# Moving the stores of the last two chunks from GpSimd's DMA queue to SyncE's

## Chip, cores, metric

One core of one Trainium2 chip. The metric is the device time in microseconds (us) of one execution. "Span" is the time from the first to the last instruction of the execution whose trace was kept; the device time is about 1.8 us longer than the span.

A DMA has "landed" when the last of the 16 DMA engines has updated its semaphore. A "DRAIN" here is an instruction that an engine's sequencer (the part that issues its instructions) runs at the program's end, before a closing barrier in which the engines wait for one another; the profile doesn't count it as busy time.

## The reference

```python
def setup_inputs():
    return {
        "pred": np.random.uniform(0.01, 0.99, (8192, 8192)).astype(np.float32),
        "target": np.random.randint(0, 2, (8192, 8192)).astype(np.float32),
    }

def reference(pred, target):
    eps = 1e-7
    pred = np.clip(pred, eps, 1 - eps)
    return -(target * np.log(pred) + (1 - target) * np.log(1 - pred))
```

It reads 537 MB and writes 268 MB, elementwise.

## The kernel before

The flat arrays are cut into chunks, and a chunk into 128 rows, one for each partition. `ring_p` and `ring_t` are rings of 32768 columns, two big chunks. A chunk is loaded whole. It is computed in pieces, in place in `ring_p`, and stored whole; only the last two chunks (`k >= tail`) are stored piece by piece. Loads of `target` cast float32 to bfloat16. Every DMA but the very first load of `pred` is issued by GpSimd.

```python
RING = 32768
BIG = 16384

def plan(total):
    head = [(8192, [4096, 4096]), (8192, [8192])]
    tail = [(8192, [4096, 4096]), (8192, [4096, 2048, 1024, 1024])]
    n = (total - sum(w for w, _ in head + tail)) // BIG
    chunks = head + [(BIG, [BIG // 2] * 2)] * n + tail
    ...
    return chunks, len(chunks) - len(tail)
# ... (tiles, dram(), span()) ...
    def load(k):
        queue = nc.sync if k == 0 else nc.gpsimd
        nc.gpsimd.dma_start(out=span(ring_t, cols[k], widths[k]), in_=dram(target_f, k))
        queue.dma_start(out=span(ring_p, cols[k], widths[k]), in_=dram(pred_f, k))

    def store(k, off, w):
        nc.gpsimd.dma_start(
            out=dram(out_f, k)[:, off : off + w], in_=span(ring_p, cols[k] + off, w)
        )

    def front(col, w):   # VectorE: clip, then (t - 1) + p; ScalarE: Abs, Ln
        ...
    def back(col, w):    # VectorE: times -1
        ...
    def finish_one():
        nonlocal stored
        k, off, w = waiting.pop(0)
        back(cols[k] + off, w)
        if k >= tail:
            store(k, off, w)
        elif off + w == widths[k]:
            store(k, 0, widths[k])
        else:
            return
        stored = cols[k] + off + w
        load_what_fits()
# ... (the loop: front() of a piece, then finish_one() of the piece before) ...
```

## Time and profile before

| | before |
|---|---|
| device time, median | 1871.96 us (1871.66 to 1872.73, 3 runs) |
| span of the traced execution | 1868.4 us (it took 1870.21 us, less than the 3 timed runs) |
| busy: VectorE (DVE), ScalarE (ACT) | 60%, 48% |
| DMA engines | 9 tenths or more in 39 of 40 slices |
| last store: issued, landed | 1852.85, 1863.37 us |
| closing DRAIN of GpSimd: from, to | 1852.83, 1867.70 us |

From the page of the kernel before: busy time, DMA in 40 slices (tenths), and the DMA queues. q0 is the software queue, which GpSimd feeds; q1 is the hardware queue, which SyncE feeds here.

```profile
DVE 1121.7 (60%) x208; ACT 899.7 (48%) x140; POOL 63.5 (3%) x109
...
DMA  9999999999999999999999999999999999999998
...
q0 software_dynamic: 15120, 666.90, 99.3%
q1 hardware_dynamic: 144, 4.19, 0.6%
```

The 16 DMA engines bound the kernel from start to end; compute has slack. So a change at the end can only act on how the end runs out.

The end of the timeline of the kernel before (start, duration, instruction):

```profile
1851.86 0.69 DVE L96 TENSOR_SCALAR ring_p<-ring_p 128x1024 f32<-128x1024 f32 x1 [1.61 <-ACT ring_p L92]
1852.85 0.53 POOL L79 DMA_DIRECT2D out_dram<-ring_p  x1 [1.77 <-DVE ring_p L96]
```

Nothing that the timeline counts happens after 1853.4 us, but the span ends at 1868.4. Ten of these 15 us are the transfer of the backlog of stores. For the rest one has to ask for the line of the program's end, L165 (count, duration in ns min/median/max, first and last start; a "q" after an engine's name means its sequencer):

```profile
L165 POOLq DRAIN  x3: 51/96/14875, 1852.8 to 1868.2; - x3
L165 SPq DRAIN  x3: 7/7/7, 1863.4 to 1868.0; - x3
```

One of GpSimd's closing DRAINs takes 14.875 us; SyncE's take 7 ns. And the waits of SyncE's queue (total us, times, longest):

```profile
SPq L165 <- DMA out_dram<-ring_p: 1862.1, 5, 1852.5
SPq L165 <- PEq L165: 4.8, 2, 4.4
```

SyncE waits for the stores, and then 4.4 us more in an end-of-program barrier. The view names PE there; the raw records of the trace show that GpSimd came last:

```
(us, the raw instruction records of before; DMA landing = 16th semaphore update)
1852.83  GpSimd DRAIN              14.875
1863.37  last store lands (all 16 DMA engines)
1863.49  Sync   DRAIN  0.007       SyncE reports to the barrier
1867.75  GpSimd EVENT_SEMAPHORE    the barrier goes on, after the DRAIN
1868.44  end of span
```

### The profile page before, as it was taken

How to read it: one execution, taken by the hardware profiler on the slowest of the kernel's cores; microseconds unless marked ns; L12 is line 12 of the kernel's file. 1: busy time of each engine (PE TensorE's matmuls, PEld its weight loads, DVE VectorE, ACT ScalarE, POOL GpSimd, SP SyncE). 2: the span in 40 equal slices, each digit the busy share in tenths (PEclk: the TensorE clock that was granted, in tenths of full speed). 3: DMA queues.
4: the chain of work that ended last, by engine and by line, in shares of the span. 5: the costliest groups of instructions: out<-in, count | busy, mean ns of one | idle time of the engine just before them, and what ended most of it. 6: DMA issues, size and time to landing. Idle time of an engine off the chain costs nothing.

```text
span 1868.4 us, 607 instructions
## 1 busy us (share of the span) xinstructions
DVE 1121.7 (60%) x208; ACT 899.7 (48%) x140; POOL 63.5 (3%) x109
## 2 busy tenths in 40 slices
DVE  4557665476654766547665566655666556675575
ACT  3355433554335543355533555335553345533465
POOL 1000000000000000000000000000000000000001
DMA  9999999999999999999999999999999999999998
GB/s 303 359 348 337 356 396 370 349 345 338 400 382 337 354 340 387 395 340 341 351 379 392 353 340 342 380 393 353 349 338 368 399 356 345 349 354 397 371 337 346
DMA packets 15268, 671.13 MB, mean 359 GB/s; under 512 B 1696, under 2 KB 1696, under 8 KB 1952
## 3 DMA queue, kind: packets, MB, share of 16 engines
q0 software_dynamic: 15120, 666.90, 99.3%
q1 hardware_dynamic: 144, 4.19, 0.6%
q14 instruction: 4, 0.03, 0.0%
HBM read 536.87 MB, written 268.44 MB: 431 GB/s over the span
## 4 chain that ended last, share of the span: by engine, by line
DMA 33%; issue 25%; ACT 24%; DVE 15%; POOL 1%; POOLq 0%; DVEq 0%; PEldq 0%
DMA ring_p<-in_pred_dram 31%; ACT ring_p L92 12%; ACT ring_p L91 12%; DVE ring_p L88 8%; DVE ring_p L85 4%; DVE ring_p L96 4%; DMA out_dram<-ring_p 1%; DMA ring_t<-in_target_dram 1%; POOL out_dram L79 1%; POOL ring_t L75 0%; POOLq L165 0%; POOLq L79 0%; DVEq L88 0%; PEldq L165 0%; POOLq L76 0%
## 5 line engine op out<-in xcount | busy, mean ns | idle before, releaser
L91 ACT ACTIVATE ring_p<-ring_p 128x8192 f32<-128x8192 f32 (+3 forms) x69 | 450.4, 6528 | 949.2 <-DVE ring_p L88 949.2
L88 DVE SCALAR_TENSOR_TENSOR ring_p<-ring_t,ring_p 128x8192 f32<-128x8192 bf16 (+3 forms) x69 | 557.1, 8074 | 2.5 <-DMA ring_t<-in_target_dram 0.2
L85 DVE TENSOR_SCALAR ring_p<-ring_p 128x8192 f32<-128x8192 f32 (+3 forms) x69 | 283.9, 4114 | 384.4 <-DMA ring_p<-in_pred_dram 384.4
L96 DVE TENSOR_SCALAR ring_p<-ring_p 128x8192 f32<-128x8192 f32 (+3 forms) x69 | 284.1, 4117 | 343.1 <-ACT ring_p L92 343.1
L92 ACT ACTIVATE ring_p<-ring_p 128x8192 f32<-128x8192 f32 (+3 forms) x69 | 450.9, 6535 | 2.2
L79 POOL DMA_DIRECT2D out_dram<-ring_p x38 | 27.4, 721 | 876.1 <-DVE ring_p L96 876.1
L76 POOL DMA_DIRECT2D ring_p<-in_pred_dram x33 | 17.6, 534 | 912.8 <-DMA out_dram<-ring_p 912.8
L75 POOL DMA_DIRECT2D ring_t<-in_target_dram x34 | 18.7, 549 | 0.8 <-PEq L165 0.8
L126 ACT ACT_TABLE_LOAD x1 | 1.3, 1283 | 0.7 <-PEq L154 0.7
L125 DVE MEMSET warm<- 1x8 f32 x1 | 0.1, 65 | 0.8 <-PEq L154 0.8
L126 ACT ACTIVATE warm<-warm 1x8 f32<-1x8 f32 x1 | 0.2, 208 | 0.0
L154 POOL MEMSET const-float32-0.0<- 128x1 f32 x1 | 0.1, 98 | 0.2 <-issue 0.2
L154 POOL MEMSET const-bfloat16-1.0<- 128x1 bf16 x1 | 0.1, 101 | 0.0
L154 POOL MEMSET const-float32-1.0<- 128x1 f32 x1 | 0.1, 98 | 0.0
L154 POOL MEMSET const-uint8-127<- 128x1 uint8 x1 | 0.1, 98 | 0.0
## 6 DMA issues: line engine op xcount, KB each, us to landing
ring_t<-in_target_dram POOLq DMA_DIRECT2D x30, 4096.0 KB, 50.0
ring_p<-in_pred_dram POOLq DMA_DIRECT2D x3, 4096.0 KB, 37.4
ring_t<-in_target_dram POOLq DMA_DIRECT2D x4, 2048.0 KB, 29.3
out_dram<-ring_p POOLq DMA_DIRECT2D x2, 4096.0 KB, 35.9
out_dram<-ring_p POOLq DMA_DIRECT2D x3, 2048.0 KB, 15.9
ring_p<-in_pred_dram SPq DMA_DIRECT2D x1, 4096.0 KB, 19.5
out_dram<-ring_p POOLq DMA_DIRECT2D x1, 1024.0 KB, 12.8
out_dram<-ring_p POOLq DMA_DIRECT2D x2, 512.0 KB, 11.1
```

The source lines that it names most:

```text
L75: nc.gpsimd.dma_start(out=span(ring_t, cols[k], widths[k]), in_=dram(target_f, k))
L76: queue.dma_start(out=span(ring_p, cols[k], widths[k]), in_=dram(pred_f, k))
L79: nc.gpsimd.dma_start(out=dram(out_f, k)[:, off : off + w], in_=span(ring_p, cols[k] + off, w))
L85: nc.vector.tensor_scalar(out=p, in0=p, scalar1=EPS, scalar2=1 - EPS, op0=Alu.max, op1=Alu.min)
L88: nc.vector.scalar_tensor_tensor(out=p, in0=t, scalar=1.0, in1=p, op0=Alu.subtract, op1=Alu.add)
L91: nc.scalar.activation(out=p, in_=p, func=Act.Abs)
L92: nc.scalar.activation(out=p, in_=p, func=Act.Ln)
L96: nc.vector.tensor_scalar(out=p, in0=p, scalar1=-1.0, scalar2=None, op0=Alu.mult)
L125: nc.vector.memset(warm, 1.0)
L126: nc.scalar.activation(out=warm, in_=warm, func=Act.Ln)
L154: nc = _bacc.Bacc("TRN2", target_bir_lowering=False, num_devices=1)
```

## The change

As the diff shows it: the stores of the last two chunks go out on another queue, SyncE's. The last two pieces become one.

```diff
-    tail = [(8192, [4096, 4096]), (8192, [4096, 2048, 1024, 1024])]
+    tail = [(8192, [4096, 4096]), (8192, [4096, 2048, 2048])]
@@
     def store(k, off, w):
-        nc.gpsimd.dma_start(
+        queue = nc.sync if k >= tail else nc.gpsimd
+        queue.dma_start(
             out=dram(out_f, k)[:, off : off + w], in_=span(ring_p, cols[k] + off, w)
         )
```

## The prediction

> **What bounds the kernel now.** The 16 DMA engines: the page's 40 slices show DMA at 9 tenths in all but the last, DVE busy 60%, ACT 48%. The change touches only the six stores of the last two chunks, so nothing before about 1812 us (the last full-chunk store) can move. In the tail I read three things.
>
> 1. *Data.* The DMA view shows 405 to 442 GB/s from 1812 to 1850. The raw packet records give 16 KB packets 611 ns, 8 KB 309, 4 KB 159. On the slowest DMA engine the last landings follow without a gap: big store 1843.9, tail stores 1848.7, 1853.6, 1858.4, 1860.9, 1862.1, 1863.4. Each step is eight packets of that engine (8 x 611 ns = 4.9 us), so its queue is never empty; the last store is issued at 1852.85 and lands 10.6 us later.
> 2. *Compute.* The timeline ends with VectorE at 1852.5, 11 us before the last byte: off the critical path.
> 3. *Closing.* SyncE sees the last landing and is done at 1863.5. But GpSimd's closing DRAIN starts at 1852.83 and takes 14.88 us, to 1867.71: 4.3 us after the last landing. The final barrier waits for it (in the waits of SyncE's queue, 4.4 us for an end-of-program barrier). Then come 0.7 us; the span is 1868.4.
>
> **What the change does.** Six stores leave GpSimd's software queue (0.53 to 2.03 us to issue each), and five go out on SyncE's hardware queue (its one load now: 0.37 us to issue, first packet 1.0 us after the issue began). The last two stores of 512 KB become one of 1 MB. The instruction order shows nothing else moved on GpSimd; SyncE's extra waits are for loads that landed by about 1825.
>
> Piece by piece:
> - Issue time saved: up to 2 us per store, behind a backlog: worth 0.
> - Merge: 8 x 309 against 16 x 159 ns per engine, -0.07 us. The last piece is ready later (1.22 + 2.29 + 1.89 + 1.91 + 1.22 us; estimate 1853.3 against 1852.5), behind a backlog that lasts to about 1861: 0.
> - Rate: the same 16 engines. The Trainium skill ("DMA: Bandwidth & Descriptors", section "Issuing engines are not separate DMA queues") says DMAs from any engine interleave on them; the trace agrees at the head, where 32 KB packets take a median of 1226 ns on the hardware and 1213 on the software queue. The tail stores will interleave with the big store, which lands later (estimate 1847 to 1850 instead of 1844); nothing waits for it. The sum is unchanged: last landing about 1863.4.
> - DRAIN: GpSimd's last transfer is now the big store. If DRAIN waits for the software queue's transfers plus about 4.3 us, it ends at about 1852 to 1854, hidden under the remaining stores. That takes 4.3 us off the critical path, less about 0.1 for the handover.
>
> **Time.** 1871.96 - 4.2 = 1867.8 us, range 1866.0 to 1870.8; faster by over 2%: 0.003, within 2%: 0.99, slower: 0.007. A gain of about 0.2%.
>
> **To check.** DRAIN starts near 1813 and ends before the last landing; last landing within 1 us of 1863.4; span ends under 1 us after it; the hardware queue carries 12.6 MB; the big store lands later; VectorE and ScalarE unchanged up to 1845.
>
> **What would make it wrong.** A closing cost of the same kind on SyncE; DRAIN's 4.3 us not tied to the software queue; slower or smaller packets in hardware-queue stores; or, on the good side, the straggling DMA engines (last landings spread over 4.3 us) being evened out by the other queue.

## The result

| | before | after |
|---|---|---|
| median | 1871.81 us (1871.09 to 1872.73, 4 runs) | 1866.78 us (1866.26 to 1868.51, 4 runs) |
| span, traced execution | 1868.4 | 1864.5 |
| last landing of the software queue | 1863.37 | 1847.14 |
| end of GpSimd's closing DRAIN | 1867.70 | 1851.23 |
| last landing of all | 1863.37 | 1863.59 |
| from last landing of all to end of span | 5.1 us | 0.9 us |

The ratio is 0.9974, 95% interval 0.9957 to 0.9992. A ratio is the mean time of one kernel's fast runs over the mean of the other's fast runs of the same rounds, so it is not quite the ratio of the medians quoted. The interval lies below 1.

The page of the kernel after, the lines that answer to those of before:

```profile
DVE 1121.4 (60%) x205; ACT 899.3 (48%) x138; POOL 58.4 (3%) x103
...
DMA  9999999999999999999999999999999999999999
...
q0 software_dynamic: 14256, 658.51, 98.5%
q1 hardware_dynamic: 864, 12.58, 1.6%
```

The hardware queue now carries 12.58 MB. The DMA engines are as full as before. The end of the timeline of after:

```profile
1828.77 25.23 SPq L80 DMA_DIRECT2D out_dram<-ring_p  x5
...
1852.41 1.23 DVE L97 TENSOR_SCALAR ring_p<-ring_p 128x2048 f32<-128x2048 f32 x1 [2.78 <-ACT ring_p L93]
```

The five stores of SyncE stand in one line, from 1828.77 to 1854.0. The line of the program's end (now L166), and the waits of SyncE's queue:

```profile
L166 POOLq DRAIN  x3: 51/96/38492, 1812.7 to 1864.2; - x3
L166 SPq DRAIN  x3: 7/7/7, 1863.7 to 1864.0; - x3
```

```profile
SPq L166 <- DMA out_dram<-ring_p: 9.2, 3, 4.4
SPq L166 <- PEq L166: 0.6, 2, 0.5
```

The DRAIN has become longer, 38.5 us, and costs nothing. It starts at 1812.73, behind GpSimd's last store, and ends at 1851.23, long before the last byte. The wait in the closing barrier went from 4.8 to 0.6 us. That 4.2 us is the gain; the data came no sooner (1863.59 against 1863.37).

### The profile page after: what moved, and what is told of

It is laid out like the page before. It is cut to its first block, busy times and chain, and to the rows that moved or that the text cites. A ratio compares the mean times of both kernels' runs of the same rounds, so it can differ in the third digit from the quotient of the medians.

```text
span 1864.5 us, 601 instructions
## 1 busy us (share of the span) xinstructions
DVE 1121.4 (60%) x205; ACT 899.3 (48%) x138; POOL 58.4 (3%) x103
## 3 DMA queue, kind: packets, MB, share of 16 engines
q1 hardware_dynamic: 864, 12.58, 1.6%
## 4 chain that ended last, share of the span: by engine, by line
DMA 33%; issue 25%; ACT 24%; DVE 15%; POOL 1%; POOLq 0%; DVEq 0%; PEldq 0%
DMA ring_p<-in_pred_dram 31%; ACT ring_p L93 12%; ACT ring_p L92 12%; DVE ring_p L89 8%; DVE ring_p L86 4%; DVE ring_p L97 4%; DMA out_dram<-ring_p 1%; DMA ring_t<-in_target_dram 1%; POOL out_dram L80 1%; POOL ring_t L75 0%; POOLq L80 0%; DVEq L89 0%; PEldq L166 0%; POOLq L76 0%; POOLq L75 0%
## 5 line engine op out<-in xcount | busy, mean ns | idle before, releaser
L92 ACT ACTIVATE ring_p<-ring_p 128x8192 f32<-128x8192 f32 (+2 forms) x68 | 450.2, 6621 | 950.1 <-DVE ring_p L89 950.1
L89 DVE SCALAR_TENSOR_TENSOR ring_p<-ring_t,ring_p 128x8192 f32<-128x8192 bf16 (+2 forms) x68 | 556.9, 8190 | 2.5 <-DMA ring_t<-in_target_dram 0.2
L86 DVE TENSOR_SCALAR ring_p<-ring_p 128x8192 f32<-128x8192 f32 (+2 forms) x68 | 283.7, 4172 | 384.7 <-DMA ring_p<-in_pred_dram 384.7
L97 DVE TENSOR_SCALAR ring_p<-ring_p 128x8192 f32<-128x8192 f32 (+2 forms) x68 | 283.9, 4176 | 344.3 <-ACT ring_p L93 344.3
L93 ACT ACTIVATE ring_p<-ring_p 128x8192 f32<-128x8192 f32 (+2 forms) x68 | 450.7, 6628 | 2.2
L80 POOL DMA_DIRECT2D out_dram<-ring_p x32 | 22.3, 696 | 842.7 <-DVE ring_p L97 842.7
## 6 DMA issues: line engine op xcount, KB each, us to landing
ring_p<-in_pred_dram POOLq DMA_DIRECT2D x30, 38.4
```

Source lines behind the costliest of these rows:

```text
L80: queue.dma_start(out=dram(out_f, k)[:, off : off + w], in_=span(ring_p, cols[k] + off, w))
L86: nc.vector.tensor_scalar(out=p, in0=p, scalar1=EPS, scalar2=1 - EPS, op0=Alu.max, op1=Alu.min)
L89: nc.vector.scalar_tensor_tensor(out=p, in0=t, scalar=1.0, in1=p, op0=Alu.subtract, op1=Alu.add)
L92: nc.scalar.activation(out=p, in_=p, func=Act.Abs)
L93: nc.scalar.activation(out=p, in_=p, func=Act.Ln)
L97: nc.vector.tensor_scalar(out=p, in0=p, scalar1=-1.0, scalar2=None, op0=Alu.mult)
```

## The experiments

Theory ("DRAIN theory"): GpSimd's closing DRAIN lasts until some 4 us after the last landing of the software queue, and the change only makes that landing come early. Rivals: the merge of the last two stores (A); the hardware queue's issue or rate (B), all at the last store or a share for each store moved (B'); something particular to SyncE (C); a closing cost on whichever engine issues the last stores (D). Each run was timed against the kernel before on the same chip.

### The merge alone

```diff
-    tail = [(8192, [4096, 4096]), (8192, [4096, 2048, 1024, 1024])]
+    tail = [(8192, [4096, 4096]), (8192, [4096, 2048, 2048])]
```
(against before)

> Only the merge of the last two 512 KB stores into one of 1 MB; all stores stay on GpSimd. DRAIN theory (the closing DRAIN on GpSimd ends about 4.2 us after the last landing of the software queue): no gain, ratio to before 1.000 (within 0.0005), DRAIN ends at about 1867.9 us, last landing 1863.4 to 1863.6, span about 1868.5. Rival A (the merge shortens the tail): ratio 0.997, as the whole change.

Measured: ratio 0.9999 (0.9987 to 1.0012), last landing 1863.09, DRAIN ends at 1867.38, span 1868.1. The merge is worth nothing; rival A falls.

### The queue alone

```diff
-    tail = [(8192, [4096, 4096]), (8192, [4096, 2048, 2048])]
+    tail = [(8192, [4096, 4096]), (8192, [4096, 2048, 1024, 1024])]
```
(against after)

> All six tail stores on SyncE, the last two not merged. DRAIN theory: the whole gain, ratio 0.997 to 0.998, span about 1864.4, DRAIN ends at about 1851, last landing about 1863.5. Rival A (the merge): ratio 1.000. Rival B (a store gains by being on the hardware queue, in issue or in rate): the whole gain as well.

Measured: ratio 0.9977 (0.9965 to 0.9990), span 1864.0, DRAIN ends at 1850.74, last landing 1863.12. The queue is the whole gain.

### Only the very last store on SyncE

```diff
-        queue = nc.sync if k >= tail else nc.gpsimd
+        queue = nc.sync if k == len(chunks) - 1 and off + w == widths[k] else nc.gpsimd
```

> The plan of after, but only the very last store goes out on SyncE; the other four tail stores stay on GpSimd. The last store overtakes the backlog of the software queue, so I expect the last landing of the software queue to stay at about 1863.5 on the slowest engine. DRAIN theory: DRAIN ends at about 1867.7, span about 1868.4, ratio 1.000, even though the last store issued is on the hardware queue. Rival B (hardware queue for the last issued store is what counts, as its issue is the last thing on the path): the whole gain, 0.997. Rival B' (each store moved gains its share): about 0.9995.

Measured: ratio 1.0000 (0.9987 to 1.0012). The last store, issued at 1853.92 on SyncE, landed at 1863.22 and so overtook the software queue, whose last store (issued 1850.18) landed at 1863.84. DRAIN ended at 1868.08, span 1868.8. That the last issued store is on the hardware queue is not enough; what counts is when the software queue lands last.

### Only the very last store on GpSimd

```diff
-        queue = nc.sync if k >= tail else nc.gpsimd
+        queue = nc.sync if k >= tail and not (k == len(chunks) - 1 and off + w == widths[k]) else nc.gpsimd
```

> The plan of after with all tail stores on SyncE but the very last, which stays on GpSimd. It alternates with the backlog of the hardware queue and should land at about 1862; last landing of all still about 1863.5. DRAIN theory: DRAIN ends about 4.2 us after the landing of that one store, at about 1866, span about 1866.8, ratio about 0.999: most of the gain is lost by one store of 1 MB. Rival B' (a share for each store moved): about 0.9975, span about 1865.3.

Measured: ratio 1.0001 (0.9987 to 1.0014). I had expected to keep some of the gain; none was kept. The store landed at 1862.90, not at about 1862, and DRAIN ended at 1867.02, that is 4.12 us later. The last landing of all was on the hardware queue, at 1863.09: that the software queue does not land last is no help either, when it lands only 0.2 us earlier. SyncE's waits and the closing DRAINs of this kernel:

```profile
SPq L166 <- DMA out_dram<-ring_p: 13.2, 1, 13.2
SPq L166 <- PEq L166: 4.4, 2, 4.0
```

```profile
L166 POOLq DRAIN  x3: 51/102/13612, 1853.4 to 1867.5; - x3
```

The barrier wait is back at 4.4 us with four of five stores moved. One late store on the software queue takes away everything; B' (a share for each) falls. The exact landing of a store that alternates with another queue was the mis-estimate here.

### The last chunk's three stores on SyncE, the two before on GpSimd

```diff
-        queue = nc.sync if k >= tail else nc.gpsimd
+        queue = nc.sync if k == len(chunks) - 1 else nc.gpsimd
```

> The two stores of the last chunk but one on GpSimd, only the last chunk's three on SyncE. The last software landing should fall between 1853.6 and 1858.5. DRAIN theory: DRAIN ends 4.2 us after it, at 1858 to 1862.7, before the last landing of all at about 1863.6: the whole gain, ratio 0.9975, span about 1864.4. Rival B' (a share for each store moved): 3 of 5 of the gain, ratio 0.9985.

Measured: ratio 0.9981 (0.9968 to 0.9995), span 1864.3. The last software landing was at 1858.78 (a little later than expected), DRAIN ended at 1862.94, the last landing of all came at 1863.37. DRAIN is hidden by 0.4 us, and its barrier wait is 0.6 us as in after. The interval does not tell 0.9981 from the 0.9985 of B'; the end of the DRAIN in the trace does.

### ScalarE's queue instead of SyncE's

```diff
-        queue = nc.sync if k >= tail else nc.gpsimd
+        queue = nc.scalar if k >= tail else nc.gpsimd
```

> The tail stores go out on ScalarE's queue instead of SyncE's. DRAIN theory: what matters is that they are off the software queue, so the whole gain: ratio 0.9975, span about 1864.4, DRAIN on GpSimd ends at about 1851. Rival C (something particular to SyncE): less gain. Rival D (the closing cost goes with whichever engine issued the last stores): a closing DRAIN of some us on ScalarE after the last landing and no gain.

Measured: ratio 0.9978 (0.9966 to 0.9991), span 1865.0, last landing 1864.11, DRAIN ends at 1851.75. C and D fall: either hardware queue will do, and the closing cost does not move to the engine that issues (ScalarE's closing DRAINs took 152 and 8 ns).

### The last big store on SyncE too, and a late DRAIN

```diff
-        queue = nc.sync if k >= tail else nc.gpsimd
+        queue = nc.sync if k >= tail - 1 else nc.gpsimd
@@ (at the end)
+        c = (cols[-1] + widths[-1] - 8) % RING
+        nc.gpsimd.tensor_copy(out=warm, in_=ring_p[0:1, c : c + 8])
```

> As after, with the last big store on SyncE too, so that the software queue's last transfer is a load that lands at about 1825; and GpSimd does one tiny copy that waits for VectorE's last result, so that its DRAIN starts at about 1854, some 29 us after that landing. If the 4.2 us are counted from the last software landing, the late DRAIN finds nothing to do and takes under 0.5 us. If they are a fixed price of a DRAIN that follows software-queue transfers, counted from its start, it takes about 4.2 us (to about 1858). The time is as after in both cases, ratio 0.9975, as both end before the last landing at about 1863.6; the length of the DRAIN decides.

Measured: ratio 1.0040 (1.0026 to 1.0054), slower than before, and DRAIN took neither 0.5 nor 4.2 us but 8.29, from 1866.48 to 1874.77. It began 25 us after the last software landing (1841.43) and ended 4.45 us after the last landing of all (1870.32), so it held the barrier again (5.0 us in the waits of SyncE). Both expectations missed, and for two reasons.

First, the time. The big store no longer queued behind the loads of the last chunk but shared the DMA engines with them, and the load that compute waits for landed at 1841.43 instead of 1824.75. VectorE sat idle for it, and the DMA engines ran out of work. From the timeline and the windows (us, busy of VectorE, ScalarE, GpSimd, clock, DMA share, GB/s) of this kernel:

```profile
1841.46 2.29 DVE L86 TENSOR_SCALAR ring_p<-ring_p 128x4096 f32<-128x4096 f32 x1 [13.33 <-DMA ring_p<-in_pred_dram]
```

```profile
1829.00:1850.00 21.00, 8.51 (x3) 5.67 (x3) 0.00 (x0) 1.00 0.78 337
```

In after the same stretch has a DMA share of 0.97 and 417 GB/s.

Second, the DRAIN. That it starts late and still takes long means that it is not a fixed delay counted from the landing: the work is done when the DRAIN runs. The table under "What the DRAIN's length goes with" suggests what the work is.

### All stores on SyncE

```diff
-        queue = nc.sync if k >= tail else nc.gpsimd
+        queue = nc.sync
```

> All stores of the whole program on SyncE, the loads stay on GpSimd. DRAIN theory: the end gains as in after (no DRAIN after the last landing). In the middle a store no longer queues behind loads but alternates with them: the loads of pred that compute waits for (38 us now) may take longer and stores too, with the DMA engines full as before. I expect a ratio between 0.996 and 1.010, with no closing wait in any case. A theory that stores are better served by the hardware queue expects clearly under 0.9975.

Measured: ratio 1.0451 (1.0437 to 1.0466), slower by 4.5%, outside my range. The closing wait is gone as expected (0.7 us in the barrier), but the middle lost far more. The wait of VectorE for `pred` grew by 98.0 us, from 384.4 to 482.4, and the span by 87.8 (from 1868.4 to 1956.2). That of GpSimd's loads for stores grew from 912.8 to 1412.0, but this is no measure of the loss: in before GpSimd also waited 876.1 us for VectorE ahead of its stores. The waits of this kernel, its times from issue to landing (loads of `pred`, then stores), and one stretch of its middle:

```profile
POOL ring_p L76 <- DMA out_dram<-ring_p: 1412.0, 26, 62.4
...
DVE ring_p L86 <- DMA ring_p<-in_pred_dram: 482.4, 26, 33.4
...
DMA to landing us min/median/max: 13.9/33.3/94.0
...
DMA to landing us min/median/max: 4.2/39.7/45.5
```

```profile
900.00:1300.00 400.00, 214.35 (x37) 176.61 (x26) 14.98 (x14) 1.00 0.97 348
```

The wait of VectorE, the loads of `pred` and the same stretch of before:

```profile
DVE ring_p L85 <- DMA ring_p<-in_pred_dram: 384.4, 31, 19.4
...
DMA to landing us min/median/max: 19.1/38.4/77.9
...
900.00:1300.00 400.00, 242.16 (x42) 196.07 (x28) 11.20 (x21) 1.00 1.00 360
```

In before GpSimd issues a store and right behind it the next load of `target` (1754.54 and 1755.07 us), so the store goes first. Here that order is lost: a load of `target` was issued at 907.08 us and the store at 913.06. Store and loads then share the DMA engines, and a store takes a median of 39.7 us to land instead of 31.3. A load of `pred` is issued only when a store has freed its columns, so it starts later. Once issued it was quicker, not slower (median 33.3 us instead of 38.4; the 94.0 and the 77.9 us are one load each, at the program's start). This account is read from the traces; no run tested it.

### What the DRAIN's length goes with

From nine traces without a late copy I set the time from the last software landing to the end of the DRAIN against the number of software-queue DMAs of the program (raw records):

```
kernel            software DMAs   last software landing -> end of DRAIN, us   us / DMA
all stores SyncE        67                    2.78                            0.0415
after                   99                    4.09                            0.0413
queue alone             99                    4.08                            0.0413
ScalarE's queue         99                    4.09                            0.0413
only last GpSimd       100                    4.12                            0.0412
two early GpSimd       101                    4.17                            0.0412
only last SyncE        103                    4.25                            0.0412
merge alone            104                    4.29                            0.0412
before                 105                    4.33                            0.0412
```

The 8.29 us of the late DRAIN, with 98 software DMAs, is twice 98 x 0.0413 us and 0.2 us for the copy. So the 4.2 us looked like about 41 ns for each software-queue DMA of the whole program. (Each of these DMAs makes 144 packets, 15120 for 105 and 9648 for 67, so the nine traces can't tell a price for each DMA from one for each packet.) The next four runs tested this.

### A late copy in the kernel after

```diff
@@ (at the end, against after)
+        c = (cols[-1] + widths[-1] - 8) % RING
+        nc.gpsimd.tensor_copy(out=warm, in_=ring_p[0:1, c : c + 8])
```

> The kernel after, with a tiny GpSimd copy at the end that waits for VectorE's last result, so that the DRAIN starts at about 1853.7, some 6.5 us after the last software landing (1847.1). In the earlier run with a late copy the DRAIN took 8.29 us from its start, with 98 software DMAs: twice 98 x 0.0413 us and 0.2 us. If the price is paid when the DRAIN runs, and twice when a copy stands before it, DRAIN takes about 0.2 + 2 x 4.09 = 8.4 us and ends at about 1862.1, before the last landing (1863.6): ratio 0.9975 as after. If the copy has nothing to do with it and a late DRAIN waits for the last landing of all queues plus 4.4 us, it ends at about 1868 and the gain is gone, ratio 1.000.

Measured: DRAIN took 8.37 us from 1856.06 to 1864.43 (0.18 + 2 x 4.09 = 8.36), 14.93 us after the last software landing (1849.49) and before the last landing of all (1865.95). Ratio 0.9979 (0.9964 to 0.9994). The price is paid when the DRAIN runs, and twice in the two runs where a GpSimd copy stands before it; why twice stays open, and no run has a late DRAIN without a copy. (This traced execution ran about 2.4 us late throughout its tail, so instants are shifted against after's.)

### The big store on SyncE without the copy

```diff
-        queue = nc.sync if k >= tail else nc.gpsimd
+        queue = nc.sync if k >= tail - 1 else nc.gpsimd
```

> The earlier run with the last big store on SyncE, without the copy: the last software transfer is a load. In that run the load that the last chunk waits for landed 16.9 us later than in after (1841.4 against 1824.5), as the big store no longer queued behind it, and the last store landed at 1870.3. I expect the same here: last landing about 1870.3, DRAIN ends at about 1841.4 + 98 x 0.0413 = 1845.5, span about 1871.1, so 4.4 us less than with the copy; ratio about 1.0015. If the copy itself had delayed the tail, the span returns to about 1864.4, ratio 0.9975.

Measured in the trace: the load landed at 1842.72, the last store at 1871.60, DRAIN ended at 1846.76, which is 4.04 us (98 x 0.0413) after that load, and the span was 1872.5. So the late load, not the copy, delays the data, and the traced execution fits. The time does not fit as well: ratio 1.0040 (1.0023 to 1.0058), because the other three executions have spans of 1878.6 to 1879.6. Where they lost 6 us more is not known; no trace of them was kept. (The 1824.5 in the expectation is the landing in before; in after it was 1824.75.)

### More software DMAs: target loads split in two

```diff
-        nc.gpsimd.dma_start(out=span(ring_t, cols[k], widths[k]), in_=dram(target_f, k))
+        t, src = span(ring_t, cols[k], widths[k]), dram(target_f, k)
+        for lo in range(0, P, P // 2):
+            nc.gpsimd.dma_start(out=t[lo : lo + P // 2], in_=src[lo : lo + P // 2])
```

in the kernel before:

> The kernel before, with each load of target issued as two DMAs of 64 partitions each: the same bytes and the same row lengths, but 139 software-queue DMAs in the program where there were 105. In the runs so far the time from the last software landing to the end of the closing DRAIN was 2.78 us with 67 software DMAs, 4.09 with 99, 4.33 with 105: about 0.0413 us for each. Count theory: DRAIN ends 139 x 0.0413 = 5.74 us after the last landing, 1.4 us more than before, and the span is about 1.4 us longer (ratio about 1.0008, if the loads land as before). Rival (a constant of about 4.2 us, or a cost of the stores alone): 4.1 to 4.4 us, ratio 1.000.

and in the kernel after:

> The kernel after, with the same split of the target loads: 133 software DMAs where there were 99. Count theory: DRAIN ends 133 x 0.0413 = 5.5 us after the big store's landing, so at about 1852.7, still hidden under the remaining stores: ratio 0.9975, the same as after, and 5.5 us faster than the split kernel with its tail on GpSimd. Rival (the split itself slows the loads): slower than after by as much as the other split kernel is slower than before.

Measured: both are slower than before by 1.1% (ratios 1.0113 and 1.0111), as the split itself slows the stream: the stores drift by about 0.8 us per chunk, and the 32 KB packets of the target loads take a mean of 2495 ns instead of 2432 between 900 and 1300 us. That was not expected. The tails say more. In the split kernel before, DRAIN ended only 0.78 us after the last landing (1889.32), not 5.74; in the split kernel after it ended 0.53 us after the big store's landing, not 5.5. The closing DRAINs and the barrier wait of the split kernel before:

```profile
L167 POOLq DRAIN  x3: 51/96/11991, 1878.1 to 1890.6; - x3
```

```profile
SPq L167 <- PEq L167: 1.2, 2, 0.7
```

So the count as I had stated it, over the whole program, is wrong. A price for each packet is wrong as well (15664 software packets in the split kernel before, against 15120). But 0.78 us is 19 x 0.0413 and 0.53 is 13 x 0.0413, and 139 and 133 are 120 more than 19 and 13. It is as if some 120 DMAs had been settled earlier and DRAIN only did the rest. This was found after the fact, from two runs, with no run left to test it; why 120 is not known.

The pair gives one more result. Where DRAIN has little to do at the end, moving the tail stores to SyncE is worth nothing: 1892.67 us with the tail on GpSimd, 1892.49 with it on SyncE (from the last landing to the end of the span there are only 1.5 and 0.9 us, so 0.6 us to gain). In the unsplit kernels the same move is worth 3.6 to 5.0 us. That is what the DRAIN theory asks for, and no theory of faster stores.

## Why the prediction was right

The prediction of 1867.8 us (1866.0 to 1870.8) holds the measured 1866.78. Step by step:

- *Data, last landing about 1863.4.* Measured 1863.59. The transfers stayed bound by the same 16 engines: 16 KB packets take 611 ns and 8 KB packets 309 ns on either queue.
- *Compute off the path, issue time worth nothing, merge worth nothing.* Shown by the merge alone (0.9999) and by the unchanged landing.
- *The big store lands at 1847 to 1850.* Measured 1847.14, from 1843.86.
- *DRAIN hidden, ending at 1852 to 1854.* It ended at 1851.23, 0.8 us before that range, as it took 4.09 us after the landing and not 4.3; the span ended 0.9 us after the last landing, as predicted.
- *The size.* Predicted 4.2 us, measured 1871.81 - 1866.78 = 5.0 between medians and 3.9 between the traced spans. The three other variants that hide the DRAIN (queue alone, ScalarE's queue, two early on GpSimd) have ratios of 0.9977, 0.9978 and 0.9981, that is 3.6 to 4.3 us of 1871. So 4.2 is about right, and the difference from 5.0 is within the scatter: after's own four runs spread over 2.3 us.
- *"If DRAIN waits for the software queue's transfers plus about 4.3 us".* The landing part is shown. The constant is not one: it was 2.78 us with 67 software DMAs, 4.09 to 4.33 with 99 to 105, and under 0.8 with 133 and 139. This step of the prediction was right for this kernel only, and for a reason that I didn't know.
- *The skill's rule.* The Trainium skill ("DMA: Bandwidth & Descriptors", section "Issuing engines are not separate DMA queues") says that starting DMAs from several engines at once only saves the sequencer's time for starting them. For the rate the trace agrees (equal packet times). For the kernel's end it is incomplete: the engine also decides whether GpSimd's closing DRAIN has to wait for the last stores (4.8 against 0.6 us in the barrier).

No variant tried beats the kernel after clearly. The queue alone, ScalarE's queue and the two-early variant are within its interval.

## What to carry to other kernels

When a profile ends with an idle stretch after the last landing, look at the closing instructions of every sequencer: work that no engine counts as busy can hold the last barrier. If the software queue's last landing comes late, its DRAIN is exposed. Let the last traffic go out on a hardware queue, all of it: here it was enough that the last software landing came 4.6 us before the last of all (two early stores on GpSimd), and one store that landed 0.2 us before it took the whole gain back. But move no store that still competes with loads: on a second queue it shares the DMA engines with transfers that were ordered before or behind it, and what compute waits for comes later (4.5% slower with all stores moved, 0.4% with one big store too many).

## What the Trainium skill lacked or had wrong

- "VectorE: DVE Perf Modes", section "The DRAIN you can't avoid", tells two kinds of DRAIN apart: one after every VectorE operation, and the runtime's boilerplate ones of about 12 ns on all five engines. It lacks the closing DRAIN of this program (L165 in before), which took 7 ns on SyncE but 14.88 us on GpSimd, 4.33 of them after the last byte had landed.
- "DMA: Bandwidth & Descriptors" has nothing on a closing cost of the software queue. The runs show 2.78 us for 67 software DMAs and 4.33 for 105 (about 41 ns each), and 0.78 for 139; with a GpSimd copy in front, 8.37 us for 99.
- The same page, section "Issuing engines are not separate DMA queues", tells that DMAs of different engines interleave, but not what this can cost a kernel. Here moving all stores to SyncE made it 4.5% slower (1954.95 us), with stores taking a median of 39.7 us to land instead of 31.3.
- The same page, section "Rules for kernel authors", advises against splitting a transfer into two partition halves, as they share the same engines. The runs agree that it doesn't help, and add a price: 34 target loads so split cost 1.1% (1892.67 against 1871.85 us).
